# Two branch projections of a decoder trunk, rebuilt from seven half-size products each and moved behind all gates

## The chip, the cores and the metric

One core of a Trainium2 chip runs the whole kernel. The metric is device time in microseconds (us). TensorE (PE) multiplies matrices into PSUM; VectorE (DVE), ScalarE (ACT) and GpSimd (POOL) do the elementwise work; SyncE (SP), ACT and POOL issue the transfers between HBM and SBUF, each from a queue of its own. Every engine works through its own list of instructions in order, and waits where an operand of the next one isn't there yet.

## The reference

One layer of a hybrid decoder trunk, with 1024 tokens and a model width of 1024, in float32:

```
h = RMSNorm(x);  P = h @ W_in
y_0 = RWKV-7 recurrence over P   (8 heads x 64)
y_1 = stick-breaking attention   (8 heads x 64)
y_2 = cross attention into 256 memory tokens (4 heads x 128)
merged = sum_b sigmoid(G_b) * (y_b @ W_br[b])     b = 0, 1, 2
x += merged @ W_out
x += ConvFFN(RMSNorm(x))
```

Each `y_b` is 1024 tokens x 512, each `W_br[b]` 512 x 1024, and the gates `G_b` are 3 x 1024 columns of P. The change concerns the lines with `merged` for b = 1 and 2.

## The kernel before

All tensors lie transposed, 128 features on the partitions and 1024 tokens along the free dimension. Matrix products keep float32 accuracy by splitting each operand into a high part (an ACT copy to the type fp32r) and a low part (a subtraction on DVE or POOL), and by three matmuls in place of one: high x high, high x low, low x high. PE works on up to 128x128 weights and 512 columns at a time, and a matmul stands in the profile as one LDWEIGHTS (PEld) and one MATMUL of `mmul`, line 139.

The program is written as Python generators, and their interleaving sets PE's order. A *main* generator (a recurrence, an attention) is woven with a *filler* stream of projections: `weave(main, filler, ratio)` advances the main part by one step and the filler by `ratio` units on average. A unit of filler is what stands between two of its `yield`s, most often six matmuls. `pinned` keeps an instruction in program order on its engine, and while `strict` is set, each pinned instruction also comes behind the pinned one before it on that engine. What isn't pinned (the copies that end a gate, most weight splits, stores) is placed by the scheduler.

The part that the change rewrites is the strict part, in which the main generator is `stage2`, the recurrence over 16 chunks of 64 tokens. Each chunk has three thirds, each one step: A makes small products for eight heads, which DVE copies (L656); B multiplies these by the chunk's inverse, and ACT copies the results (L664); C makes the output, copied by ACT (L676), and the new state, updated by DVE (L674). Each third needs the copies of the third before it. After chunks 3, 7, 11, 13 and 15 (counted from zero) `norm_part` adds the group norm in pieces to the following steps: reductions on DVE (L699, L700), squares on ACT (L706, four a step, 16 for a part of two groups and 8 for a part of one), a power on POOL (L195), and scalings on DVE (L715). `group_norm` follows with the ratio 1.0: it transposes on PE (`turn`, L729 and L730 on DVE) and splits the result (L734 on ACT, L735 on DVE). Then comes `branch_last`, the projection for b = 0.

The filler in that part: `gate_item` (eight units of six matmuls; `fin` copies on ACT L885 and scales on DVE L886; the sigmoid L889 is put off to the next item's unit by `close_gates`, and the gate goes to HBM in `gsd`), and `branch_item` (four units; DVE multiplies the product by the gate, L1297; for b = 2 POOL adds the sum so far, L1299; POOL issues the store to `mrd`, L1300). The mark `y1`, three gates after the memory attention, starts it. Before, 20 of the 24 gates go to HBM and four stay on the chip beside their branch item; the items after the mark are the eight of branch 1, one gate with the splits of branch 2's operand, the eight of branch 2 with a gate before each of the last four, and two gates. Gates and old sums share three buffers of the tag `w4`; loads come from SP (L1283, L1286).

The later parts that the change touches: in `up_phase`, the up projection, which is already made with seven products of half size for eight, `act_sums` adds activation blocks on DVE (the tile `gall`); in `down_phase`, `complete` adds finished output blocks (L1874) at the start of each group of steps; in `sb_qk`, `k_split` copies the keys' halves.

## Time and profile before

| | us |
|---|---|
| median of three runs (lowest, highest) | 1789.28 (1788.69, 1789.63) |
| profiled execution, own time | 1788.33 |
| its span, first to last instruction | 1786.6 |
| PE busy in the span | 1774.7 |
| DVE / ACT / POOL busy | 1185.1 / 883.3 / 698.3 |

The span is 1.7 us shorter than the profiled execution's own time; the rest lies around the instructions. Stretches of the profile are given in us from the span's start. The strict part with the recurrence runs from about 779 to 985, the group norm to about 1009, the up projection to about 1490, and the down projection to the end. PE's busy time counts overlapping matmuls once; the start-to-start distance of the matmuls is their cost.

### The profile page before, as it was taken

To read this page: it belongs to the slowest core of one execution; us is meant where nothing else is said; L and a number is where in the kernel's file an instruction comes from. 1 tells how busy PE (TensorE), PEld (TensorE's weight loads), DVE (VectorE), ACT (ScalarE), POOL (GpSimd) and SP (SyncE) were. 2 spreads that over 40 slices of the span, in tenths; PEclk is the share of its full clock that TensorE was granted. 3 is DMA by queue.
4 is the path that set the end of the run, shared out by engine and by line. 5 is a ranking of instruction groups with operands and counts; after the bars stand their busy time and mean duration, and the time that the engine had idled before them with its cause. 6 is when DMAs were issued, how large, how long until landed. Compare 5 with 4: busy or idle time off the path is not lost.

```text
span 1786.6 us, 27452 instructions
## 1 busy us (share of the span) xinstructions
PE 1774.7 (99%) x10481; PEld 1442.4 (81%) x10481; DVE 1185.1 (66%) x1687; ACT 883.3 (49%) x1667; POOL 698.3 (39%) x409
## 2 busy tenths in 40 slices
PE   9999999999999999999999999999999999999999
PEld 7777778878888888787777888887888888888887
DVE  5666674787888655243533873698767777795597
ACT  6544344566566635444546434454444445445343
POOL 1233252222231012122433321257777677535454
PEclk9999999999999999999999999999999999999999
DMA  4256574111112333658763653323323333396475
GB/s 185 74 166 193 181 244 148 51 57 42 54 57 77 103 126 93 203 181 278 269 228 145 230 211 105 108 89 124 101 89 104 115 104 113 109 329 224 142 246 202
DMA packets 120757, 263.39 MB, mean 147 GB/s; under 512 B 28329, under 2 KB 41129, under 8 KB 120498
## 3 DMA queue, kind: packets, MB, share of 16 engines
q1 hardware_dynamic: 82434, 193.31, 33.1%
q10 hardware_dynamic: 34416, 55.72, 8.5%
q0 software_dynamic: 3776, 12.62, 2.3%
q8 instruction: 82, 1.34, 0.3%
q14 instruction: 49, 0.40, 0.1%
HBM read 180.04 MB, written 81.53 MB: 146 GB/s over the span
## 4 chain that ended last, share of the span: by engine, by line
PE 61%; issue 1%; DVE 1%; POOL 1%; ACT 1%; DMA 1%; ACTq 0%; DVEq 0%; POOLq 0%; SPq 0%
PE mm L139 53%; PE g L139 8%; PE g L122 1%; POOL dw L1854 1%; DMA vmd<-w 0%; ACT wh L83 0%; DMA qk<-vd 0%; DVE qk L715 0%; ACT w L885 0%; DVE gall L1646 0%; DVE w L886 0%; DVE ga L1635 0%; DVE keep L1874 0%; DVE g L1629 0%; DVE g L1630 0%
## 5 line engine op out<-in xcount | busy, mean ns | idle before, releaser
L89 POOL TENSOR_TENSOR wl<-wr,wh 128x1024 fp32r<-128x1024 f32 x58 | 147.8, 2550 | 368.2 <-ACT wh L83 355.0
L139 PE MATMUL mm<-xhi,wh 128*128 128x512 f32 x784 | 260.5, 413 | 1.4 <-ACT xhi L222 1.0
L139 PE MATMUL mm<-xlo,wh 128*128 128x512 f32 x784 | 243.6, 392 | 0.1
L139 PE MATMUL mm<-xhi,wl 128*128 128x512 f32 x784 | 242.2, 390 | 0.0
L139 PEld LDWEIGHTS mm<-xlo,wh 128*128 128x128 f32 x784 | 147.0, 188 | 33.4 <-DVE xlo L225 1.0
L139 PEld LDWEIGHTS mm<-xhi,wl 128*128 128x128 f32 x784 | 147.2, 188 | 32.7
L139 PEld LDWEIGHTS mm<-xhi,wh 128*128 128x128 f32 x784 | 136.6, 189 | 31.1 <-issue 7.9
L139 PE MATMUL mm<-dw,da 128*128 128x512 f32 x528 | 120.9, 390 | 0.0
L83 ACT ACTIVATE wh<-wr 128x1024 fp32r<-128x1024 f32 x75 | 79.5, 1060 | 81.5 <-PE mm L139 57.2
L139 PE MATMUL mm<-BT,l 128*128 128x512 f32 x504 | 117.9, 389 | 0.3 <-POOL l L1555 0.3
L139 PEld LDWEIGHTS mm<-dw,da 128*128 128x128 f32 x528 | 98.9, 188 | 21.3 <-DVE da L1853 0.8
L1854 POOL TENSOR_TENSOR dw<-draw,dw 128x512 fp32r<-128x512 f32 x55 | 83.6, 1530 | 76.1 <-ACT dw L1852 74.2
L985 DVE TENSOR_TENSOR_SCAN at<-at,at 128x128 f32<-128x128 f32 (+3 forms) x64 | 91.0, 1428 | 33.1 <-ACT at L979 33.0
L139 PEld LDWEIGHTS mm<-BT,l 128*128 128x128 f32 x504 | 94.5, 188 | 20.3 <-POOL l L1555 0.7
L139 PE MATMUL mm<-BT,wh 128*128 128x512 f32 x352 | 108.6, 390 | 1.7 <-DVE u L1685 1.7
L139 PE MATMUL mm<-B,wh 128*128 128x512 f32 x352 | 108.6, 389 | 0.0
L195 POOL TENSOR_TENSOR hf<-rs,half 128x16 f32<-128x16 f32 (+1 forms) x18 | 49.2, 2734 | 142.2 <-DVE rs L192 137.8
L1853 DVE TENSOR_TENSOR da<-draw,da 128x512 fp32r<-128x512 f32 x77 | 66.9, 877 | 49.1 <-ACT da L1851 48.8
L139 PE MATMUL g<-dw,da 128*128 128x512 f32 x396 | 90.6, 389 | 0.4 <-POOL dw L1854 0.4
L1851 ACT ACTIVATE da<-draw 128x512 fp32r<-128x512 f32 x77 | 48.3, 628 | 80.7 <-PE mm L139 29.9
L139 PEld LDWEIGHTS g<-dw,da 128*128 128x128 f32 x396 | 74.2, 188 | 16.2 <-POOL dw L1854 0.8
L1555 POOL TENSOR_TENSOR l<-it,l 128x1024 fp32r<-128x1024 f32 x20 | 48.0, 2402 | 85.5 <-ACT l L1554 85.5
(343 smaller groups left out, 3972.1 us busy)
## 6 DMA issues: line engine op xcount, KB each, us to landing
wr<-in_w_in_dram SPq DMA_DIRECT2D x49, 512.0 KB, 3.7
draw<-actd SPq DMA_DIRECT2D x77, 256.0 KB, 3.3
at<-scr SPq DMA_DIRECT2D x28, 512.0 KB, 5.6
draw<-in_w_down_dram SPq DMA_DIRECT2D x55, 256.0 KB, 4.8
rw<-in_w_up_dram SPq DMA_DIRECT2D x22, 512.0 KB, 3.6
actd<-gall ACTq DMA_DIRECT2D x41, 256.0 KB, 3.4
gsd<-w ACTq DMA_DIRECT2D x20, 512.0 KB, 2.7
wr<-in_w_up_dram SPq DMA_DIRECT2D x18, 512.0 KB, 3.6
```

What stands on the lines that cost most here:

```text
L83: ins = self.nc.scalar.activation(hi, raw, AF.Copy)
L89: self.last_wl = self.nc.gpsimd.tensor_tensor(lo, raw, hi.bitcast(F32), ALU.subtract)
L122: self.pinned(self.nc.tensor.transpose(out, in_, self.ident[:n, :n]))
L139: self.pinned(self.nc.tensor.matmul(*a, **k))
L195: nc.gpsimd.tensor_tensor(out, t[:, :n], self.half[:, :n], ALU.pow)
L985: self.pinned(nc.vector.tensor_tensor_scan(sn[:, :W][:, ::-1], sn[:, :W][:, ::-1], self.smask[:, 1024 - W :][:, ::-1], 1.0, ALU.mult, ALU. ...
L1555: self.last_low = keep(eng.tensor_tensor(lo, src, hi.bitcast(F32), ALU.subtract))
L1851: self.pinned(nc.scalar.activation(A[:, 0], a, AF.Copy))
L1853: self.pinned(nc.vector.tensor_tensor(A[:, 1], a, A[:, 0].bitcast(F32), ALU.subtract))
L1854: nc.gpsimd.tensor_tensor(Wt[:, 1], w, Wt[:, 0].bitcast(F32), ALU.subtract)
```

## The change

For a pair of row blocks (256 output features) and one branch, the old code makes two blocks of 128 features x 1024 tokens with K = 512. The new `branch_pairs` cuts the pair's weight into four blocks `a11, a12, a21, a22` (by half of K and by row block) and the operand `y` into four blocks by half of K and half of the tokens, and makes the four output blocks from seven products of half size (2 k x 3 = 6 matmuls of 512 columns each) for eight. It needs sums of weights (on POOL: three per pair ahead, and `a12` minus a sum later), sums of operand blocks (on DVE, four of 128x1024 per branch), the splits of seven operands per branch (14 for two, where eight tiles were split), splits of each product's weight (56 of 256 columns, high on ACT and low on POOL, seven products ahead), a copy of the first product out of PSUM on ACT, and joins of the products on DVE. All of these are pinned. `st["t"]` and `st["o"]` hold joins and old sums; `xt` gives the operands the buffers of `xhi` and `xlo`, which the last gate frees piece by piece.

The order becomes: all seven gates left behind the mark `y1`, the last two with hooks (`hooks1`, `hooks2`) that make the operands of branch 1 and the first weights; then 56 products, one unit each. Branch 2's operands are made during products 21 to 31. The filler ratio goes from 2.08 to 1.92. All 24 gates now go to HBM, and each product pair loads its two gates back.

Also: the copies in `k_split` come behind the last copy that ends a gate; the memory keys take two `at` buffers in place of `w4`; in the up projection the activation sums of one pair move from the end of its own third product and the next pair's sixth to the next pair's sixth and seventh; in the down projection the additions after the group with i = 7 (done in the group with i = 4) are spread over every second step, 0 to 6, and the stores come at step 8.

```diff
...
     def t4(self, tag="w4", dt=F32, n=1024):
...
+
+    def xt(self, name, dt=F32R):
+        return self.pool_x.tile([128, 1024], dt, name=self.nm(name), tag="xt", bufs=16)
...
     def ps(self, tag="g"):
...
-        self.xhi, self.xlo = ([self.pool_x.tile([128, 1024], F32R, name=f"x{n}{k}") for k in range(8)] for n in ("hi", "lo"))
+        self.xhi, self.xlo = zip(*[[self.xt(f"x{n}{k}") for n in ("hi", "lo")] for k in range(8)])
...
         def load(eng, tile, src):
...
-        self.rbc = self.pool_x.tile([128, 1024], F32, name="rbc")
+        self.rbc = self.pool_x.tile([128, 1024], F32, name="rbc", tag="rbc", bufs=1)
...
-            nc.scalar.activation(K[i][q], kr[q], AF.Copy)
-            nc.scalar.activation(K[i][o], kr[q], AF.Copy)
+            for x in (q, o):
+                self.behind(nc.scalar.activation(K[i][x], kr[q], AF.Copy), self.last_fin)
...
-                st["k"] = self.t4(), self.t4()
+                st["k"] = self.t4("at"), self.t4("at")
...
-    def load_y(self, b, st):
...
     def branch_mm(self, d, w, y, out, k):
...
-    def branch_item(self, b, d, st, first):
...
-    def branch(self, b, first):
...
+    def branch_pairs(self):
+        nc = self.nc
+        act = lambda *a, **k: self.pinned(nc.scalar.activation(*a, **k))
+        vec = lambda o, a, b, op: self.pinned(nc.vector.tensor_tensor(o, a, b, op))
+        gps = lambda o, a, b, op: self.pinned(nc.gpsimd.tensor_tensor(o, a, b, op))
+        f = lambda x: x.bitcast(F32)
+        two = lambda x: x.rearrange("p (k t) -> p k t", k=2)
+        N, L, R = 8, slice(0, 512), slice(512, 1024)
+        seq = [(0, 1)]
+        for n in range(N):
+            seq += [(n, 6), (n, 2), (n, 5), (n, 7), (n, 4)] + ([(n + 1, 1)] if n + 1 < N else []) + [(n, 3)]
+        at = {x: s for s, x in enumerate(seq)}
+        st, Y, W, S, G, bank, wh, wl, raws, early = {}, {}, {}, {}, {}, {}, [], [], {}, []
+
+        def load_y(b, tiles):
+            raws[b] = [two(t) for t in tiles]
+            for q, (k, t) in zip(raws[b], ((0, L), (0, R), (2, L), (2, R))):
+                nc.sync.dma_start(f(q), self.yd[b, k : k + 2, :, t].rearrange("k p t -> p k t"))
+
+        def load_first():
+            load_y(1, [self.t4("A", dt) for dt in (F32, F32, F32, F32R)])
+
+        def operands(b):
+            q11, q12, q21, q22 = raws[b]
+            if b == 1:
+                st["big"] = self.pool_a.tile([128, 4, 1024], F32R, name="yhi", tag="inst")
+            big = [two(st["big"][:, j]) for j in range(4)]
+            new = lambda dt=F32R: two(early.pop(0) if early else self.xt("y", dt))
+            low = lambda: two(self.t4("A", F32R)) if b == 1 else new()
+            sub = lambda o, x, y: vec(o, x, y, ALU.subtract)
+
+            def split(i, q, hi, lo):
+                act(hi, f(q), AF.Copy)
+                sub(lo, f(q), f(hi))
+                Y[b, i] = hi, lo
+
+            yield split(1, q11, big[0], big[1])
+            yield sub(q11, q12, q11)
+            yield split(2, q21, big[2], big[3])
+            t2 = st["t2"] = new(F32)
+            sub(t2, f(q22), q11)
+            yield sub(q21, t2, q21)
+            yield split(6, t2, new(), new())
+            yield split(5, q11, new(), new())
+            yield sub(q12, f(q22), q12)
+            yield split(7, q12, new(), low())
+            hi4, hi22 = new(), new()
+            yield split(4, q21, hi4, low())
+            yield split(3, q22, hi22, q22)
+
+        def tiles(*dts):
+            early.extend(self.xt("y", dt) for dt in dts)
+
+        def begin():
+            st["y"] = operands(1)
+            next(st["y"])
+
+        def load_w(n):
+            if n < N:
+                W[n] = self.load_w(self.I["w_br"][1 + n // 4, n % 4])
+
+        def quads(n):
+            w = W[n].rearrange("p (a k m c) -> p m a k c", a=2, k=2, m=2)
+            return w[:, 0, 0], w[:, 0, 1], w[:, 1, 0], w[:, 1, 1]
+
+        def weight_sums(n):
+            if n < N:
+                a11, a12, a21, a22 = quads(n)
+                s1, s2 = S[n] = [st["s"][:, n % 2 * 512 + o : n % 2 * 512 + o + 256].rearrange("p (k c) -> p k c", k=2) for o in (0, 256)]
+                gps(s1, a21, a22, ALU.add)
+                gps(s2, s1, a11, ALU.subtract)
+                gps(a21, a11, a21, ALU.subtract)
+
+        def operand(s, tile, k=None):
+            x = tile[s % 8 // 4][:, s % 4 * 256 : s % 4 * 256 + 256]
+            return x.rearrange("p (k c) -> p k c", k=2) if k is None else x[:, k * 128 : (k + 1) * 128]
+
+        def weight(s):
+            if s >= len(seq):
+                return
+            n, i = seq[s]
+            a11, a12, a21, a22 = quads(n)
+            if i == 3:
+                gps(a12, a12, S[n][1], ALU.subtract)
+            src = {1: a11, 2: a12, 3: a12, 4: a22, 5: S[n][0], 6: S[n][1], 7: a21}[i]
+            hi, lo = operand(s, wh), operand(s, wl)
+            act(hi, src, AF.Copy)
+            gps(lo, src, f(hi), ALU.subtract)
+
+        def room():
+            wh.append(self.pool_wt.tile([128, 1024], F32R, name=self.nm("wh"), tag="wh", bufs=2))
+            wl.append(self.pool_wt.tile([128, 1024], F32R, name=self.nm("wl"), tag="wl", bufs=2))
+
+        def w_first():
+            room()
+            load_w(0)
+
+        def w_next():
+            load_w(1)
+
+        def gate(n, r):
+            if n < N:
+                g = G[n, r] = self.t4()
+                nc.sync.dma_start(g, self.gsd[1 + n // 4, n % 4 * 2 + r])
+
+        def old(n, r):
+            if n < N and "o" in st:
+                nc.sync.dma_start(st["o"][n % 2 * 2 + r], self.mrd[n % 4 * 2 + r])
+
+        def put(n, r):
+            g, d = G.pop((n, r)), n % 4 * 2 + r
+            if n > 3:
+                (nc.vector if n == N - 1 else nc.gpsimd).tensor_tensor(g, g, st["o"][n % 2 * 2 + r], ALU.add)
+            nc.gpsimd.dma_start(self.mrd[d], g)
+
+        def product(s):
+            n, i = seq[s]
+            key, first = {1: ("A", True), 2: ("A", False), 6: ("B", True), 7: ("B", False), 5: ("C", True), 3: ("C", False), 4: ("D", True)}[i]
+            if first:
+                bank[n, key] = self.ps("mm")
+            o, y = bank[n, key], Y[1 + n // 4, i]
+            for k in range(2):
+                for pi, (u, v) in enumerate(((0, 0), (0, 1), (1, 0))):
+                    self.mmul(o, operand(s, (wh, wl)[u], k), y[v][:, k], start=(first and k == 0 and pi == 0),
+                              stop=(k == 1 and pi == 2), skip_group_check=not first)
+            p1 = st["t"][0][:, L] if n % 2 else st["t"][1][:, L]
+            x2, x3 = st["t"][0][:, R], st["t"][1][:, R]
+            if i == 1:
+                act(p1, o, AF.Copy)
+            elif i == 6:
+                vec(x2, o, p1, ALU.add)
+            elif i == 5:
+                g = G[n, 0]
+                vec(g[:, L], bank.pop((n, "A")), g[:, L], ALU.mult)
+            elif i == 7:
+                vec(p1, o, p1, ALU.add)
+                vec(x3, bank[n, "C"], p1, ALU.add)
+            elif i == 4:
+                vec(p1, p1, o, ALU.subtract)
+                g = G[n, 1]
+                vec(g[:, L], p1, g[:, L], ALU.mult)
+                vec(g[:, R], x3, g[:, R], ALU.mult)
+                put(n, 1)
+                gate(n + 1, 0)
+                old(n + 2, 1)
+            elif i == 3:
+                vec(x2, o, x2, ALU.add)
+                g = G[n, 0]
+                vec(g[:, R], x2, g[:, R], ALU.mult)
+                put(n, 0)
+                gate(n + 2, 1)
+                old(n + 2, 0)
+
+        def run():
+            yield
+            gate(0, 1)
+            gate(0, 0)
+            room()
+            st["t"] = [self.pool_x.tile([128, 1024], F32, name=self.nm("rbc"), tag="rbc", bufs=1), st["x"]]
+            for s in range(4, 7):
+                weight(s)
+            for s in range(len(seq)):
+                product(s)
+                n, i = seq[s]
+                weight(s + 7)
+                if s == 0:
+                    self.close_gates()
+                    gate(1, 1)
+                if s % 7 == 1:
+                    load_w(s // 7 + 2)
+                if s % 7 == 5:
+                    weight_sums(s // 7 + 2)
+                if s in (0, 2):
+                    next(st["y"])
+                if s == 1:
+                    load_y(2, [self.xt("q", dt) for dt in (F32, F32, F32, F32R)])
+                elif s == 20:
+                    st["y"] = operands(2)
+                elif 21 <= s <= 31 and s != 27:
+                    next(st["y"])
+                if s == 31:
+                    st["o"] = [x.rearrange("p k t -> p (k t)") for x in (*raws[2][:3], st["t2"])]
+                    for r in (1, 0):
+                        old(4, r)
+                        old(5, r)
+                yield
+
+        def sums_first():
+            st["x"], st["s"] = self.xt("t", F32), self.xt("s", F32)
+            weight_sums(0)
+
+        step = lambda: next(st["y"])
+        weights = lambda *ss: lambda: [weight(s) for s in ss]
+        hook = lambda *fs: lambda: [g() for g in fs]
+        hooks1 = {1: begin, 3: step, 5: step}
+        hooks2 = {0: hook(w_first, lambda: tiles(F32, F32R)), 1: hook(step, w_next, lambda: tiles(F32R, F32R)), 2: hook(step, lambda: tiles(F32R, F32R)),
+                  3: hook(step, lambda: tiles(F32R, F32R)), 4: sums_first, 5: hook(step, weights(0, 1)), 6: hook(step, weights(2, 3)), 7: lambda: weight_sums(1)}
+        return load_first, hooks1, hooks2, run()
...
     def load_wo(self, k):
...
-                if n > 2 and pairs[n - 1][2]:
-                    act_sums(pairs[n - 1][1], True)
...
-                elif pairs[n][2]:
-                    act_sums(pairs[n][1], False)
...
         def u1_first(n):
...
-                    late, part = ((False, 0), (False, 1), (True, 0), (True, 1))[(5, 6, 7, 4).index(i)]
-                    act_sums(0, late, (part,))
+                    for late, part in {5: ((False, 0),), 6: ((False, 1), (True, 0)), 7: ((True, 1),)}.get(i, ()):
+                        act_sums(0, late, (part,))
+                elif n > 3 and n % 2 == 0 and i in (6, 7):
+                    act_sums(pairs[n - 1][1], i == 7)
...
-            if f < 4:
+            if i != 4 and f < 4:
...
-            elif f == 5:
+            elif i == 4 and f < 8 and f % 2 == 0:
+                complete(f // 2)
+            elif f == (8 if i == 4 else 5):
...
-        self.stored = set(gq)
+        gq += [(2, d) for d in range(4, 8)]
...
-        ld1, br1, sp1 = self.branch(1, True)
-        ld2, br2, sp2 = self.branch(2, False)
-        items += [lambda: drain(inv), ld1, gate(sp1), gate(), gate(), mark("y1"), *br1, ld2, gate(sp2), *br2, gate(), gate()]
+        load1, hooks1, hooks2, pairs = self.branch_pairs()
+        items += [lambda: drain(inv), load1, gate(), gate(), gate(), mark("y1"), *[gate() for _ in range(5)], gate(hooks1), gate(hooks2), pairs]
...
-        self.weave(st2, pump, 2.08, 0)
+        self.weave(st2, pump, 1.92, 0)
...
```

46 lines of the change are left out of this document (1 added, 45 removed).

## The prediction

> **What bounds the kernel now.** I read the page first, then busy time by stretch, then the instructions in order of time in the stretch that the change rewrites, then the groups by form that give each price.
>
> ```profile
> span 1786.6 us, 27452 instructions
> PE 1774.7 (99%) x10481; PEld 1442.4 (81%) x10481; DVE 1185.1 (66%) x1687; ACT 883.3 (49%) x1667; POOL 698.3 (39%) x409
> 779.00:985.00 206.00, 205.28 (x2110) 161.41 (x2109) 86.28 (x245) 111.23 (x405) 67.05 (x39) 1.00 0.65 227
> 1200.00:1480.00 280.00, 278.01 (x1225) 229.58 (x1224) 210.41 (x312) 130.02 (x179) 208.20 (x121) 1.00 0.33 107
> 1480.00:1786.00 306.00, 302.39 (x1329) 248.77 (x1328) 225.55 (x280) 134.19 (x218) 163.45 (x106) 1.00 0.58 196
> ```
>
> PE is the bound: 1774.7 of 1786.6 us busy, and in the stretch 779 to 985, where both branch projections run between the thirds of the recurrence's chunks, 205.28 of 206. The clock column says 1.00 throughout. A matmul taken away saves its time if nothing else becomes late. DVE (86 us) and ACT (111 us) have room there on average; whether they have it at each step decides this change.
>
> ```profile
> 780.83 0.61 PE L139 MATMUL mm<-yhi,wh 128*128 128x512 f32 x2
> 782.19 0.61 PE L139 MATMUL mm<-yhi,wh 128*128 128x512 f32 x2
> 796.15 0.68 PE L139 MATMUL g<-ys,at 64*64 64x64 f32 x16
> 800.18 0.68 PE L139 MATMUL g<-ys,qk 64*64 64x64 f32 x16
> 803.74 0.68 PE L139 MATMUL g<-ys,at 64*64 64x64 f32 x16
> 808.40 0.56 PE L139 MATMUL g<-ys,at 64*64 64x64 f32 x12
> ```
>
> A unit of filler is six matmuls and takes 782.19 - 780.83 = 1.36 us, 0.227 each. The other rows are one chunk's thirds (A, B, C) with two units behind each: 4.03, 3.56 and 4.66 us.
>
> **The change part by part.** *Matmuls.* Two branches x 8 row blocks x 24 = 384 become 56 products x 6 = 336. 48 x 0.227 = 10.9 us saved; nothing else on PE changes.
>
> *Moved activation sums, spread additions, key buffers.*
>
> ```profile
> 1239.65 0.73 PE L139 MATMUL mm<-BT,wh 128*128 128x512 f32 x2 [1.69 <-DVE u L1685]
> 1741.88 10.99 PE L139 MATMUL g<-dw,da 128*128 128x512 f32 x47 [0.36 <-POOL dw L1854]
> ```
>
> These are the two waits there that the moved DVE work can cause. Removed, they give 2.0; not removed, 0. I take 1.5. The order of the key copies and the `at` tiles I cost at nothing, since PE's rows cover them.
>
> *What ACT and DVE get.* The prices, from two views: rows that begin with a line number are groups (busy us, mean ns of one | idle before, what ended it), rows that begin with a time are single stretches in order (start, length, in brackets the idle time before).
>
> ```profile
> L885 ACT ACTIVATE w<-mm 128x512 f32<-128x512 f32 x15 | 8.2, 593 | 0.1
> L889 ACT ACTIVATE w<-w 128x1024 f32<-128x1024 f32 x8 | 8.5, 1058 | 13.8 <-DVE w L886 13.8
> L1365 ACT ACTIVATE mg<-at 128x256 fp32r<-128x256 f32 x16 | 5.8, 408 | 2.2 <-DVE at L1359 2.2
> 777.45 2.96 ACT L1267 ACTIVATE yhi<-A 128x1024 fp32r<-128x1024 f32 x3 [0.40 <-ACT w L889]
> 886.83 0.35 ACT L706 ACTIVATE jk<-qk,hn 128x64 f32<-128x64 f32 x1 [4.09 <-DVE hn L700]
> 887.30 0.35 ACT L706 ACTIVATE jk<-qk,hn 128x64 f32<-128x64 f32 x1
> 888.71 1.86 ACT L664 ACTIVATE qk<-g 64x64 f32<-64x64 f32 x8
> L1297 DVE TENSOR_TENSOR w<-mm,w 128x512 f32<-128x512 f32 x32 | 20.5, 683 | 17.9 <-PE mm L139 13.6 <-DMA w<-gsd 4.3
> L715 DVE TENSOR_SCALAR qk<-qk,hn,hf 128x64 f32<-128x64 f32 x64 | 17.1, 336 | 0.9 <-POOL hf L195 0.9
> L674 DVE SCALAR_TENSOR_TENSOR ys<-ys,pc,g 128x64 f32<-128x64 f32 x60 | 14.5, 279 | 50.4 <-issue 25.5 <-PE g L139 25.0
> L656 DVE COPY ys<-g 128x64 f32<-128x64 f32 x64 | 9.8, 214 | 21.8 <-PE g L139 21.8
> 743.51 1.22 DVE L886 TENSOR_TENSOR w<-w,rbc 128x1024 f32<-128x1024 f32 x1 [10.27 <-ACT w L885]
> ```
>
> Back to back, ACT's 128x1024 copies take 2.96/3 = 0.99, a square 0.47 (887.30 - 886.83), eight recurrence copies 1.86. From 1.06 to 0.99 is 0.1 of overlap, so a 512 copy is 0.5 and a 256 copy (a weight's high part) 0.31. On DVE a 512 operation that reads PSUM is 0.68 (0.66 in a row), a 1024 one 1.22.
>
> In the strict part every pinned instruction keeps program order on its engine, and the new splits, copies and additions are all pinned, so a late one holds up the recurrence's copies behind it, on which the next third's matmuls wait. After the mark y1 come 7 gates of 8 units, then 56 products. At 1.92 units a step the last gate falls on steps 26 to 30 and product s on step (57+s)/1.92; the group norm's squares (four a step) sit on steps 28-31, 40-43 and 46-47 as before.
>
> *Stretch 1, steps 26-31* (thirds C A B C A B, the first with one unit). PE: 3.30+4.03+3.56+4.66+4.03+3.56 = 23.1. ACT: four sets of recurrence copies 7.4, 16 squares 7.5, four operand splits 4.0, two gates' copies 2.1 and sigmoids 2.1, eight weights 2.5, one product copy 0.5: 26.1. ACT is 3.0 behind when the next C third needs its copies; and it idles at the start, as the 4.09 in the 886.83 row shows for the same place now: the first split there waits for DVE, which has a gate's scaling, the reductions and a sum ahead of it. Ends: 1.5 (the last copies may trail) and 8; I take 3.0+4.1 = 7.
>
> *Stretch 2, steps 40-47, products 18-33.* PE 3x3.56+3x4.66+2x4.03 = 32.7. DVE: 23 joins 15.2 (nine per seven products), eleven 1024 operations for branch 2's operands 13.2, the recurrence 2x4x0.214+3x4x0.279 = 5.1, 16 scalings 5.4: 38.9, so 6.2 over. ACT: 24 squares 11.3, six sets of copies 11.2, 16 weights 5.0, seven splits 6.9, two product copies 1.0: 35.4, 2.7 over. They wait on each other (split, low part, split) and two norm parts start, each with the 4 us wait. Ends: 3 (ACT's excess alone) and 17 (both excesses and two waits); I take 12.
>
> *Stretch 3, the group norm, 15 units.*
>
> ```profile
> 986.32 1.03 PE L122 MATMUL g<-kon,qk 128*128 128x128 f32 x8
> 987.11 0.71 PE L139 MATMUL mm<-xhi,wh 128*128 128x512 f32 x2
> L729 DVE TENSOR_TENSOR at<-g,at 128x512 f32<-128x512 f32 x7 | 4.7, 684 | 1.3 <-PE g L122 1.3
> L735 DVE TENSOR_TENSOR A<-qk,qk 128x512 fp32r<-128x512 f32 x6 | 4.0, 684 | 0.1
> ```
>
> PE: 15x1.36 plus 32 transposes at 0.79 per eight, 23.6. DVE: 24 operations of 0.684 (16.4), eight scalings 2.7, 15 x 9/7 joins 12.7: 31.8, against gates there now. 8 behind, less what the last projection's start can wait. Ends 1 and 12; I take 6.
>
> *POOL and the gates' loads.*
>
> ```profile
> L1299 POOL TENSOR_TENSOR w<-w,w 128x1024 f32<-128x1024 f32 x7 | 16.6, 2378 | 25.7 <-DVE w L1297 20.6 <-DVE hn L699 3.5 <-DMA w<-mrd 1.6
> L1582 POOL TENSOR_TENSOR wr<-wr,wr 128x512 f32<-128x512 f32 x10 | 12.9, 1287 | 0.0
> L1300 POOL DMA_DIRECT2D mrd<-w x16: 531/572/616, 787.5 to 997.8; - x16
> DMA to landing us min/median/max: 2.9/5.8/7.9
> L1283 SPq DMA_DIRECT2D w<-gsd x12: 319/319/320, 765.8 to 887.1; - x12
> DMA to landing us min/median/max: 3.3/4.1/4.8
> 891.61 1.29 DVE L1297 TENSOR_TENSOR w<-mm,w 128x512 f32<-128x512 f32 x2 [4.30 <-DMA w<-gsd]
> ```
>
> POOL gets 56 low parts and 32 sums of 256 columns; no such row exists, and the line through 1.29 and 2.38 gives 0.75: 66 us over the phase. A low part is made seven products (9.5 us of PE) ahead of its use, so I cost POOL's time itself at nothing; but the high parts of four kinds in seven are taken from POOL's sums, so a late POOL makes ACT wait, in front of the recurrence's copies. Each pair's second gate loads into the buffer that the pair before stores from: three DVE joins 2.0, issue 0.57, landing 5.8, load 0.32+4.1 = 12.8, and 15.2 with the addition, against five products and two to three thirds, 6.8+3.5 = 10.3. DVE then waits 2.5 or 4.9; a 4.30 wait at 891.61 cost PE nothing. On SP a waiting gate load holds the recurrence's and the weights' next loads; the former are asked for two groups (four chunks) ahead, the latter almost two pairs, so some 5 us cost them nothing. Ends 0 and 10; I take 2. The four gates that are newly stored and read back add four store issues on ACT's queue and four loads on SP's, beside PE's work: nothing.
>
> **Sum.** -10.9 - 1.5 + 7 + 12 + 6 + 2 = +14.6. On the profiled run's 1788.33 that is 1802.9; the median, 1789.28, stands 1 us higher: 1804. All at the good ends -13 (1776); at the bad ones 8+17+12+10-10.9 = +36 (1825).
>
> **Rivals.** *Faster: the backlog is absorbed.* A recurrence copy is needed only one step later, so 2.7 us of lateness is free, and the real order of the unpinned gate copies may be kinder. If ACT and DVE never fall more than one step's two units behind in any stretch, only the saving is left: -12.4, 1777. For it: the 4.30 wait without cost. Against it: the excesses of 3 to 8 us. It decides where ACT's 26.1 us in stretch 1 shrink below 23.1+2.7.
>
> *DVE is locked out by POOL.*
>
> ```profile
> 980.33 2.40 POOL L89 TENSOR_TENSOR wl<-wr,wh 128x1024 fp32r<-128x1024 f32 x1 [9.18 <-ACT wh L83]
> 981.46 2.35 DVE L886 TENSOR_TENSOR w<-w,rbc 128x1024 f32<-128x1024 f32 x1 [8.08 <-ACT w L885]
> ```
>
> The operation that took 1.22 at 743.51 took 2.35 here: it got almost nowhere until POOL ended at 982.73. POOL would be busy some 20 of stretch 2's 32.7 us (16 low parts and 11 sums of 0.75), six tenths of it, and 19 of DVE's larger operations there (eleven for the operands, eight gate products) have both inputs in SBUF. If six tenths of them meet a POOL operation and lose 0.75 each, DVE is 8 us later: +23, 1812. [...]
>
> *The gate loads rule.* If each of the seven rounds stops PE for its wait, 4x2.5+3x4.9 = 25 in place of the stretches' delays, which would run inside those waits: -12.4+25 = +12, 1801. Against it: the 4.30 wait.
>
> **Chances.** The forecast 0.40, the lock 0.13, the gate loads 0.07 (all slower); absorbed, 0.30; half absorbed, stalls between 9 and 16 us, within 0.2% (3.6 us, about what a measurement of this kernel can tell from no change), 0.10. Faster 0.30, same 0.10, slower 0.60. The range 1776 to 1825 holds both signs; the likeliest case alone is 1796 to 1814.
>
> **What would show it.** PE's records fall by 48 and its idle time in the rewritten stretch rises from under 1 us to some 27, as waits for ACT's recurrence copies (L664, L676) near the last gate and for DVE's copies and updates around branch 2's splits; ACT over 0.9 busy there. Wrong would be: PE idle below 12 us in all, or waits that name DMA or POOL first. In the up projection the 1.69 wait should be gone.

## The result and the profile after

The changed kernel takes 1865.53 us (median of 5 runs, 1864.86 to 1867.82), the kernel before 1789.28 beside it: a ratio of 1.0426 (95% interval 1.0411 to 1.0442), 76 us slower. The forecast was 1804, with a range up to 1825: the sign was right, the size was not.

The page of the changed kernel, the whole span: busy time of each engine, and the granted clock of PE in 40 slices.

```profile
span 1863.8 us, 27582 instructions
PE 1796.1 (96%) x10433; PEld 1451.6 (78%) x10433; DVE 1266.3 (68%) x1742; ACT 900.5 (48%) x1729; POOL 753.7 (40%) x488
PEclk9999999999999999999888799999999999999999
```

PE's records fell from 10481 to 10433: the 48 matmuls are gone. The clock has a dent that the page before did not show. Busy time by stretch (start:end, length, then busy time and instructions of PE, PEld, DVE, ACT and POOL, PE's clock, DMA share, GB/s):

```profile
779.00:985.00 206.00, 186.40 (x1863) 143.78 (x1861) 102.20 (x223) 116.90 (x401) 74.21 (x71) 0.95 0.53 187
985.00:1085.00 100.00, 66.56 (x347) 51.60 (x348) 75.80 (x123) 34.39 (x103) 55.77 (x53) 0.78 0.56 197
```

Up to 985 PE idles 20 us where it idled 0.7, from 985 to 1085 another 33. The last projection, `branch_last`, starts at 1081.6 in place of 1011.8: 70 of the 76 us are lost here, in the stretch that the change rewrites. What PE waits for between 779 and 1090 (engine, tile and line <- releaser: us in total, times, longest; lines of the changed kernel: L667 and L679 are the copies of the second and last thirds, L659 DVE's copies, L1262 to L1264 the new helpers on ACT, DVE and POOL):

```profile
PE g L142 <- ACT qk L667: 14.5, 3, 7.2
PE mm L142 <- DVE rbc L1263: 11.2, 2, 6.4
PE g L142 <- DVE ys L659: 9.2, 3, 6.3
PE mm L142 <- DVE t L1263: 8.6, 2, 5.9
PE g L142 <- ACT qk L679: 7.2, 4, 5.6
```

The first large wait, beside the last gate, and the start of the last projection:

```profile
908.37 1.90 PE L142 MATMUL g<-ys,at 64*64 64x64 f32 x16 [7.23 <-ACT qk L667]
...
1081.61 1.23 PE L142 MATMUL mm<-qk,wh 128*128 128x512 f32 x4
```

Some 31 of the 51 us of waits look like the forecast's picture (ACT's and DVE's copies late), 20 are waits of the products for DVE's joins. ACT itself, in the same stretch, does not lack time (116.9 of 206 us busy, and 13.3 of 18 from 890 to 908 beside the last gate, where the forecast had over 0.9); it waits:

```profile
ACT wh L1262 <- POOL wr L1264: 57.8, 8, 11.4
ACT qk L679 <- DVE ys L677: 19.8, 11, 3.3
```

One of these eight waits in single stretches (start, length, in brackets the idle time before), POOL, ACT and PE in order of time:

```profile
1013.04 2.34 POOL L1372 TENSOR_TENSOR w<-w,q 128x1024 f32<-128x1024 f32 x1
...
1017.37 0.57 POOL L1373 DMA_DIRECT2D mrd<-w  x1
1017.96 0.74 POOL L1264 TENSOR_TENSOR wr<-wr,s 128x256 f32<-128x256 f32 x1
1018.73 0.42 ACT L1262 ACTIVATE wh<-wr 128x256 fp32r<-128x256 f32 x1 [9.38 <-POOL wr L1264]
1019.06 1.85 ACT L667 ACTIVATE qk<-g 64x64 f32<-64x64 f32 x8
1019.54 1.42 PE L142 MATMUL g<-ys,at 64*64 64x64 f32 x12 [6.20 <-ACT qk L667]
```

POOL adds an old sum, makes two weight sums and a low part of other products (the rows left out), issues the store, and only then subtracts `s2` from `a12` for the weight of the third kind. ACT has waited 9.38 us for that subtraction; the recurrence's copies stand behind the weight on ACT, and PE waits 6.20 us for the copies. POOL, which the prediction costed at nothing, is at the head of this chain. Another of PE's waits for ACT is of the same kind:

```profile
945.64 0.42 ACT L1262 ACTIVATE wh<-wr 128x256 fp32r<-128x256 f32 x1 [8.35 <-POOL wr L1264]
946.58 1.89 PE L142 MATMUL g<-ys,at 64*64 64x64 f32 x16 [5.59 <-ACT qk L679]
```

### The profile page after: what moved, and what is told of

Same layout as the page of the kernel before. It is cut to its first block, busy times and chain, and to the rows that moved or that the text cites. A ratio compares the mean times of both kernels' runs of the same rounds, so it can differ in the third digit from the quotient of the medians.

```text
span 1863.8 us, 27582 instructions
## 1 busy us (share of the span) xinstructions
PE 1796.1 (96%) x10433; PEld 1451.6 (78%) x10433; DVE 1266.3 (68%) x1742; ACT 900.5 (48%) x1729; POOL 753.7 (40%) x488
## 4 chain that ended last, share of the span: by engine, by line
PE 47%; DVE 7%; issue 5%; ACT 4%; POOL 3%; DMA 1%; SPq 0%; ACTq 0%; DVEq 0%; POOLq 0%
PE mm L142 40%; PE g L142 6%; POOL dw L1999 1%; DVE gall L1793 1%; ACT g L1774 1%; PE g L125 1%; DVE gall L1782 1%; ACT sg L1779 1%; DVE qk L718 1%; POOL wl L1264 1%; DVE qk L733 1%; DVE g L1777 1%; DVE w L1263 1%; DVE rbc L1263 0%; ACT jk L709 0%
## 5 line engine op out<-in xcount | busy, mean ns | idle before, releaser
L92 POOL TENSOR_TENSOR wl<-wr,wh 128x1024 fp32r<-128x1024 f32 x50 | 128.9, 2578 | 346.5 <-ACT wh L86 340.9
L86 ACT ACTIVATE wh<-wr 128x1024 fp32r<-128x1024 f32 x67 | 71.1, 1061 | 79.4 <-PE mm L142 74.9
L1774 ACT ACTIVATE g<-u,params 128x512 f32<-128x512 f32 x88 | 64.9, 770 | 68.8 <-DVE u L1853 63.5
```

The source lines that it names most:

```text
L86: ins = self.nc.scalar.activation(hi, raw, AF.Copy)
L92: self.last_wl = self.nc.gpsimd.tensor_tensor(lo, raw, hi.bitcast(F32), ALU.subtract)
L1774: keep(nc.scalar.activation(c, u[:, 2 + h * 512 : 514 + h * 512], AF.Identity, scale=self.par("cw2", m), bias=self.par("cb", m)))
```

## The experiments

All times below are medians (the kernel before, run beside each group, stood between 1788.9 and 1790.1, so a difference of 1 us between two groups says nothing); "the base" is the kernel of the third run, 1852.33, on which most of the others are built. Two theories were set against each other: Q, the order of POOL's queue, and L, that DVE and ACT have too much to do, as forecast, only more of it. A third, P, came up after the first four.

| run | edit | us | ratio to before, 95% interval |
|---|---|---|---|
| e1 | third-kind sum made earlier | 1856.32 | 1.0371 (1.0357, 1.0385) |
| e2 | stores issued by SP | 1861.11 | 1.0394 (1.0378, 1.0410) |
| e3 | both: the base | 1852.33 | 1.0351 (1.0337, 1.0365) |
| e4 | kernel before + small edits | 1796.08 | 1.0036 (1.0023, 1.0048) |
| e5 | base, no POOL low parts | 1841.33 | 1.0292 (1.0277, 1.0307) |
| e6 | base, low parts on DVE | 1849.21 | 1.0338 (1.0322, 1.0353) |
| e7 | base, low parts and sums on DVE | 1851.18 | 1.0348 (1.0333, 1.0363) |
| e8 | base, norm's scalings on ACT | 1851.14 | 1.0345 (1.0327, 1.0362) |
| e9 | base, no POOL arithmetic in the products | 1829.66 | 1.0220 (1.0202, 1.0238) |
| e10 | base, no DVE work for branch 2's operands | 1843.19 | 1.0299 (1.0283, 1.0315) |
| e11 | base, ratio 1.6 | 1853.21 | 1.0352 (1.0335, 1.0368) |
| e12 | base, ratio 2.3 | 1854.69 | 1.0367 (1.0348, 1.0385) |
| e13 | base, matmuls repeated at the waits | 1852.71 | 1.0352 (1.0338, 1.0366) |
| e14 | base, two of the norm's three DVE steps out | 1848.19 | 1.0328 (1.0312, 1.0344) |
| e15 | kernel before + moved activation sums | 1795.96 | 1.0034 (1.0021, 1.0046) |
| e16 | kernel before + spread additions | 1789.89 | 1.0003 (0.9995, 1.0012) |
| e17 | e9 + e10 + e14 | 1815.11 | 1.0145 (1.0128, 1.0162) |
| e18 | e17 without the gates' loads | 1802.14 | 1.0070 (1.0055, 1.0085) |

**e1, e2, e3: POOL's queue.**

```diff
-            if i == 3:
-                gps(a12, a12, S[n][1], ALU.subtract)
+            if i == 5:
+                gps(a11, a12, S[n][1], ALU.subtract)
...
-            src = {1: a11, 2: a12, 3: a12, ...
+            src = {1: a11, 2: a12, 3: a11, ...
```

> The sum a12 - s2 for the third-kind weight is made four products earlier (into a11, which is free by then), so that ACT's high part no longer waits for a POOL queue with the stores and additions of the pair before in front. Nothing else changes. Theory Q (queues: ACT waits 57.8 us in 8 waits for POOL, POOL waits for DVE's joins, and the recurrence's copies stand behind ACT's wait): most of the stalls go, PE idles below 25 us between 900 and 1085 in place of about 55, the clock there rises above 0.92, and the time is 1800 to 1820. Theory L (load: ACT and DVE simply have more to do than PE around the last gate and branch 2's operands, as the prediction had it, with terms too small): the ACT waits for POOL vanish, but PE's idle time stays above 40 us and the time is 1850 to 1866.

The second kernel leaves that as it was and moves the stores:

```diff
-            nc.gpsimd.dma_start(self.mrd[d], g)
+            nc.sync.dma_start(self.mrd[d], g)
```

> The stores of the finished pairs are issued by SP in place of POOL; POOL keeps the additions of the last three pairs. Theory Q: POOL no longer waits for DVE's joins in the first four pairs, so the first four of the eight ACT waits shrink from 3 to 8 us to below 2 each; the additions still hold POOL from pair 4 on: 1825 to 1850. Theory L: no change within 5 us of 1865. SP's loads now stand behind stores that wait for DVE: if that matters, waits that name DMA on the w4 tiles appear, and the time rises.

> Both edits. Theory Q: the earlier sum alone already uncouples ACT from the stores, so this stands within 5 us of the early sum alone. Theory L: within 5 us of 1865.

The order of the queue costs 9.2 us, the stores' place another 4.0; together 13.2, a sixth of the loss. The first two times lie 36 and 11 us above theory Q's ranges and within theory L's; the third, within 5 us of the first, is Q's, and 8 us below L's range. So Q holds for a part, not in its full form: after the first edit ACT's waits for POOL shrink from 57.8 us to 12.1 (of which none is for the third kind's sum), and PE waits for DVE instead. The rows after the first edit, PE, DVE and POOL, show by whom DVE was held:

```profile
1025.45 0.79 PE L142 MATMUL mm<-y,wh 128*128 128x512 f32 x1 [8.77 <-DVE t L1263]
1026.04 0.63 PE L142 MATMUL mm<-q,wh 128*128 128x512 f32 x1
1026.47 0.63 PE L142 MATMUL mm<-y,wl 128*128 128x512 f32 x1
...
1047.85 2.38 POOL L1372 TENSOR_TENSOR w<-w,q 128x1024 f32<-128x1024 f32 x1 [1.24 <-DVE w L1263]
1048.72 0.68 DVE L732 TENSOR_TENSOR at<-g,at 128x512 f32<-128x512 f32 x1
...
1050.70 4.73 DVE L733 TENSOR_TENSOR qk<-at,at 128x512 f32<-128x512 f32 x1
1051.12 1.44 POOL L1264 TENSOR_TENSOR wl<-wr,wh 128x256 fp32r<-128x256 f32 x2
1052.52 2.36 POOL L1372 TENSOR_TENSOR w<-w,q 128x1024 f32<-128x1024 f32 x1
```

An addition of 128x512 with both inputs in SBUF (0.69 us on average in the kernel before) took 4.73 and ended at 1055.43, 0.55 us after POOL's run of three operations. An operation of the same size that reads PSUM (the tile `g`) took 0.68 beside POOL's addition of 2.38. A DVE held by POOL is the rival that the prediction gave 13%; it became theory P. The rows also show PE's matmuls 0.43 us apart after the wait of 8.77, where 0.23 is their distance in the kernel before, at a granted clock of 1.00.

**e5 to e9: what POOL's arithmetic costs.** In e5 the low parts after the first eight are left out; e6 gives the low parts to DVE, e7 the sums too; e9 leaves out the low parts after the first eight, the sums from the third pair on, and POOL's additions of old sums.

```diff
-            gps(lo, src, f(hi), ALU.subtract)
+            if s < 8:                                   # e5, e9
+                gps(lo, src, f(hi), ALU.subtract)
+            vec(lo, src, f(hi), ALU.subtract)           # e6, e7
...
-                gps(s1, a21, a22, ALU.add)
+                vec(s1, a21, a22, ALU.add)              # e7, and the other sums
```

> From the kernel with the earlier sum and SP's stores: POOL's low parts of the weights after the first eight are left out (the old ones stay in their buffers), so the output isn't the reference's, and 48 POOL operations of 128x256 go. Everything else, DVE's and ACT's work too, stays. Theory P (POOL locks DVE out: in the trace with the earlier sum, one 128x512 group-norm addition took 4.73 us at 1050.70 in place of 0.68, ending with a run of POOL operations; such excesses over the unhindered lengths sum to some 33 us between 900 and 1085): the excess falls to below 18 us, PE idles less by 10 to 20 us, and the time is 1815 to 1840. Theory L (DVE and ACT have too much work of their own, whatever POOL does): 1846 to 1853.

> The same kernel with the 56 low parts made by DVE in place of POOL. DVE gets 56 x 0.37 = 20 us more, spread over the 56 products. Theory P: what DVE gets it wins back from the lock, 1840 to 1860. Theory L: DVE is 20 us busier in stretches where it sets the pace, 1860 to 1875.

> Low parts and weight sums all on DVE; POOL keeps the additions of old sums alone. DVE gets 31 us more. Theory P: 1838 to 1865, with DVE's excess over its unhindered lengths below 10 us. Theory L: 1868 to 1885.

> From the kernel with the earlier sum and SP's stores, like the run without low parts, but POOL's weight sums from the third pair on and its additions of old sums are left out as well (the output isn't the reference's); POOL is left with the small powers of the norm, the first splits, the transfers it issues and the last projection's splits. Theory P (the lock): DVE's operations keep their unhindered lengths up to the last projection and the time falls by as much again as without the low parts, to 1820 to 1833. Theory L (DVE's own load): within 4 us of the run without low parts, 1837 to 1845.

POOL's arithmetic costs 22.7 us (e9 against the base), the low parts alone 11.0: theory P's range holds three of the four times and misses e5 by 1 us; theory L's holds none. Moved to DVE, 20 and 31 us of added work (by the expectations' count) cost nothing on balance (-3.1 and -1.2): DVE won back about what it was given. Its groups show it; first the changed kernel, then the base, then the kernel with all of it on DVE, each from 900 to 1085:

```profile
L718 DVE TENSOR_SCALAR qk<-qk,hn,hf 128x64 f32<-128x64 f32 x48 | 21.1, 509 | 0.0
L733 DVE TENSOR_TENSOR qk<-at,at 128x512 f32<-128x512 f32 x6 | 11.3, 1891 | 0.0
```

```profile
L718 DVE TENSOR_SCALAR qk<-qk,hn,hf 128x64 f32<-128x64 f32 x48 | 15.6, 397 | 0.0
L733 DVE TENSOR_TENSOR qk<-at,at 128x512 f32<-128x512 f32 x6 | 6.7, 1127 | 0.0
```

```profile
L718 DVE TENSOR_SCALAR qk<-qk,hn,hf 128x64 f32<-128x64 f32 x48 | 11.2, 308 | 0.0
L733 DVE TENSOR_TENSOR qk<-at,at 128x512 f32<-128x512 f32 x6 | 5.6, 944 | 0.0
```

The scalings take 509, 397 and 308 ns (306 in e9, 305 in the kernel before), the additions 1891, 1127 and 944: POOL's arithmetic accounts for the second step, the first came with the order of its queue. That DVE's operations run longer beside POOL's arithmetic is shown by these rows; that all 22.7 us are this lock is not, since without POOL's work its queue and the additions between join and store are gone as well. From the base to e9 the scalings, these additions and the norm's low parts (L738) lose 8.9 us of busy time in this window.

**e8, e11, e12: the same work on another engine or at another time.**

```diff
-                self.pinned(nc.vector.tensor_scalar(y, y, nm[:, j : j + 1], rs[:, j : j + 1], ALU.add, ALU.mult))
+                self.pinned(nc.scalar.activation(y, y, AF.Identity, bias=nb[:, j : j + 1], scale=rs[:, j : j + 1]))   # e8; nb = nm * rs
...
-        self.weave(st2, pump, 1.92, 0)
+        self.weave(st2, pump, 1.6, 0)      # e11; e12: 2.3
```

> The group norm's 64 scalings made by ACT (Identity with scale and bias, some 0.35 us each) in place of DVE (19.4 us for 48 of them between 900 and 1085 where unhindered ones take 11.3). Both theories that put the stalls on DVE: 1830 to 1845. If ACT is the engine that sets the pace (its 22 us more fall where it has the squares and the recurrence's copies): 1855 to 1870.

> From the same kernel with 1.6 units of filler a step in place of 1.92: more of the recurrence and the group norm's first parts fall on the gates, where DVE is busy 50 of 121 us, fewer on the products. If DVE's joint load of joins, operands and norm is what stalls PE: 1830 to 1847. If the thirds' own latency needs the 2.6 us of filler behind each: stalls from 785 on that name the recurrence's copies, 1855 to 1880.

> From the same kernel with 2.3 units a step: the recurrence is spread over more products, fewer products beside the group norm. By the joint load the stalls get fewer in 940 to 1022 and the recurrence's end runs longer: 1845 to 1865. If the products themselves (joins, gate loads) set the pace, no change within 4 us.

All three lie within 2.4 us of the base; the first two fit neither of their expectations, the third fits both and so decides nothing. With the scalings on ACT, PE's waits for DVE's copies fall from 8.4 us in the base to 1.2 and those for the joins in `t` from 14.4 to 10.5, but those for ACT's copies, 3.4 in the base, become:

```profile
PE g L142 <- ACT qk L667: 11.8, 5, 3.9
```

Most of what DVE was relieved of, ACT charged: in this run neither engine alone sets the pace.

**e10, e14: the two loads that the prediction had costed.** In e10 `sub` does nothing for b = 2 and high parts serve as low ones; in e14 this goes:

```diff
-            sub = lambda o, x, y: vec(o, x, y, ALU.subtract)
+            sub = lambda o, x, y: vec(o, x, y, ALU.subtract) if b == 1 else None        # e10
...
-            self.pinned(nc.vector.tensor_tensor(y[:, hs], gg[:, hs], bg[:, hs], ALU.add))      # e14
...
-            nc.vector.tensor_tensor(lo[:, hs], self.y[p][:, hs], hi[:, hs].bitcast(F32), ALU.subtract)      # e14
```

> From the same kernel with DVE's eleven 128x1024 operations for branch 2's operands left out (high parts serve as low parts, unsummed blocks as sums, so the output isn't the reference's); ACT's seven copies stay. The prediction put 13.2 us of DVE work and a stall of 12 us there. Theory L: 1832 to 1843. If the stall there comes from elsewhere (the lock, the gate loads, ACT): 1848 to 1853.

> From the same kernel: the group norm's additions (eight of 128x512) and low parts (eight) on DVE are left out in the stretch after the recurrence, and high parts stand in for low ones in the last projection (the output isn't the reference's). The prediction had DVE 8 us behind PE there, and a cost of 6. If DVE's own load sets that stretch: 16 x 0.68 = 11 us and what the lock adds, 1832 to 1842. If the stalls there come from elsewhere (loads of the old sums, POOL's additions): 1847 to 1853.

They give 9.1 us, at the upper edge of theory L's range, and 4.1, which says that the stalls behind the recurrence come from elsewhere too. In the second, DVE's waits show what comes next, the gate loads: two waits in the base (first row), four without the norm's steps (second), both from 895 to 1082.

```profile
DVE w L1263 <- DMA w<-gsd: 11.2, 2, 6.1
```

```profile
DVE w L1261 <- DMA w<-gsd: 20.9, 4, 8.1
```

**e13: the slower clock.**

```diff
+            if s in (42, 46, 55):
+                idle = self.ps("g")
+                for _ in range(24):
+                    self.mmul(idle, *self.again, start=True, stop=True)
+            self.again = operand(s, wh, 0), y[0][:, 0]
...
+            for _ in range(40 if c == 14 else 0):
+                self.mmul(us[0][7][:, 256:512], self.again[0], self.again[1][:, :256], start=True, stop=True)
```

> From the kernel with the earlier sum and SP's stores: repeated matmuls, whose results nobody reads, are put in front of the four places where PE waits 6 to 8 us (the second third of the recurrence's chunk 14 and products 42, 46 and 55), 24 of 512 columns (5.4 us) or 40 of 256 (some 4.7 us) each, so that PE works in most of each wait. Theory K (the slower clock after a wait costs by itself: six matmuls take 2.55 us in place of 1.36 behind the wait that ended at 1025 in the trace with the earlier sum): the clock rises above 0.94 between 985 and 1070 and the time falls to 1838 to 1847. If DVE sets the pace there whatever PE's speed: 1850 to 1856, with PE's waits behind the added matmuls longer.

Busy time by stretch, the base and then this kernel:

```profile
985.00:1022.00 37.00, 27.51 (x214) 20.62 (x213) 19.01 (x43) 21.38 (x82) 19.73 (x19) 0.87 0.55 202
1022.00:1066.00 44.00, 26.73 (x102) 20.83 (x101) 38.51 (x51) 10.33 (x19) 26.81 (x20) 0.77 0.55 203
```

```profile
985.00:1022.00 37.00, 34.10 (x279) 27.43 (x278) 16.97 (x40) 19.70 (x78) 17.87 (x18) 0.98 0.55 200
1022.00:1066.00 44.00, 34.75 (x149) 27.82 (x150) 39.70 (x52) 11.07 (x22) 28.75 (x21) 0.95 0.55 203
```

The clock rose from 0.87 and 0.77 to 0.98 and 0.95, and the time did not move (+0.4 us). At products 42, 46 and 55 PE still waits behind the repeats (1.5, 3.6 and 2.5 us): there DVE and the loads set the pace, and a slow PE only waits less. The fourth group, in the recurrence's chunk 14, came behind its wait and held PE itself:

```profile
980.89 7.53 PE L142 MATMUL g<-y,wh 128*128 128x256 f32 x40 [6.21 <-DVE ys L659]
988.35 0.68 PE L142 MATMUL g<-ys,qk 64*64 64x64 f32 x16
```

Product 55 starts 1.3 us later than in the base, so a gain of that size from the faster clock could be hidden. Matmuls stand 0.43 us apart behind waits of 8.77 (e1), 3.17 (e18, below) and 3.62 (here, at product 46), and 0.23 apart behind the one of 1.49 at product 42. In this stretch the slower clock costs at most some 2 us of its own (an estimate: the 1.3 and the scatter of the runs).

**e4, e15, e16: the small edits on the kernel before.** The edits are those of the change itself, without `branch_pairs`; the first has all of them, the others one each:

```diff
-                if n > 2 and pairs[n - 1][2]:
-                    act_sums(pairs[n - 1][1], True)                  # e15
...
+                elif n > 3 and n % 2 == 0 and i in (6, 7):
+                    act_sums(pairs[n - 1][1], i == 7)                # e15
...
-            if f < 4:
+            if i != 4 and f < 4:
                 complete(f)
+            elif i == 4 and f < 8 and f % 2 == 0:
+                complete(f // 2)                                     # e16
```

> The kernel before with the small edits alone (order of the key copies, key buffers, moved activation sums, spread additions), without the seven-product branches. The prediction has -1.5: 1787.5 to 1788.2. By the changed kernel's trace, where the up projection's small waits for DVE's u sum to 4.3 us and 1.5 more for POOL's l while the one of 1.69 is gone, they cost 1 to 4 us: 1790 to 1793.

> The kernel before with the moved activation sums alone. The four small edits together cost 6.0 us. By the trace of those, where DVE's u makes eight waits in place of one and POOL's l one more, nearly all of it is this: +3 to +6, 1792 to 1796. By the prediction: -1.7, 1787.6.

> The kernel before with the spread additions of the down projection alone. By the trace of the four small edits PE's busy time after 1480 changed by 1.3 us: within 1.5 us of before, 1788 to 1791. By the prediction -0.4.

The small edits cost 6.0 us, more than either reading had; the moved activation sums alone 6.0, the spread additions nothing. PE's waits with the moved sums alone, the largest two:

```profile
PE mm L139 <- DVE u L1618: 4.4, 8, 0.6
PE mm L139 <- POOL l L1555: 1.5, 1, 1.5
```

The one wait of 1.69 has become eight of up to 0.6, and one of POOL's grew from 0.3 to 1.5: 3.9 us of the 6.0. The other 2 have no row; PE's busy time is longer too, 1778.0 us where the page of the kernel before has 1774.7 for the same 10481 matmuls, and why stays open.

**e17, e18: all at once.** e17 joins e9, e10 and e14. e18 also leaves the gates' loads out:

```diff
-                g = G[n, r] = self.t4()
-                nc.sync.dma_start(g, self.gsd[1 + n // 4, n % 4 * 2 + r])
+                G[n, r] = self.t4()
...
-                vec(g[:, L], bank.pop((n, "A")), g[:, L], ALU.mult)
+                vec(g[:, L], bank.pop((n, "A")), f(st["big"][:, 0])[:, L], ALU.mult)
```

> From the kernel with the earlier sum and SP's stores, three things left out at once: POOL's low parts, sums and additions, DVE's operations for branch 2's operands, and DVE's additions and low parts of the group norm (the output isn't the reference's). If the causes add up: 1852.3 - 22.7 - 9.1 - 4.1 = 1816. If they cover each other and the gate loads come last: DVE waits over 20 us for gate loads between 900 and 1050 and the time is 1810 to 1825. If they cover each other without the gate loads: 1785 to 1808, with DVE's waits for loads below 12 us.

> The same without the gates' loads: the products are multiplied by another tile that stays on the chip, and the buffer that takes the result is still the one that the pair before stores from. If the gate loads were the last bound: within 6 us of the floor, 1789.5 + 6.0 (small edits) - 10.9 (48 matmuls) = 1785, with PE's waits between 900 and 1050 below 8 us. If a cause without a name is left: over 1797.

The three parts add up: 37.2 us together, 35.9 one by one (22.7 + 9.1 + 4.1). That the gate waits would grow past 20 us was wrong (11.8 us in four, PE's waits 16 in all), but their loads are worth 13.0 us once the rest is gone. What is left in e18, 17.5 us above the floor of 1784.6 (1789.5 + 6.0 - 10.9), is only partly named: as its expectation says for a time over 1797, a cause without a name is left. PE's waits, and the rows around the largest (one of ACT among them):

```profile
PE g L142 <- ACT qk L667: 3.6, 2, 3.2
PE mm L142 <- DVE t L1261: 1.7, 2, 1.5
PE g L142 <- DVE ys L659: 1.4, 1, 1.4
```

```profile
904.38 1.85 ACT L667 ACTIVATE qk<-g 64x64 f32<-64x64 f32 x8
904.86 1.90 PE L142 MATMUL g<-ys,at 64*64 64x64 f32 x16 [3.17 <-ACT qk L667]
906.69 1.97 PE L142 MATMUL g<-qk,at 128*64 128x64 f32 x32
...
910.89 0.63 PE L142 MATMUL mm<-y,wl 128*128 128x512 f32 x1
911.32 0.63 PE L142 MATMUL mm<-y,wh 128*128 128x512 f32 x1
...
912.59 0.40 PE L142 MATMUL mm<-A,wh 128*128 128x512 f32 x1
912.83 0.40 PE L142 MATMUL mm<-y,wl 128*128 128x512 f32 x1
913.15 0.56 PE L142 MATMUL g<-ys,at 64*64 64x64 f32 x12
```

This is the wait beside the last gate. Behind it the products' matmuls stand 0.43 us apart (910.89, 911.32), and 0.24 at 912.59; the granted clock is 0.91 from 900 to 940, with 1.00 in the stretches before and behind. Here PE is the bound again, so that costs: by the distances of the rows some 3.4 us (an estimate: 1.2 and 0.8 on the two groups of the third, 7 matmuls by 0.2). A part of the 1.2 may belong to ACT's eight copies, which run beside that group and which it needs. The pages bound the rest: against the kernel with the small edits (span 1794.3, PE busy 1778.8) e18 (1799.1 and 1774.8) has 8.8 us more idle time of PE and, with 10.9 of matmuls gone, 6.9 more busy time than these leave. Waits of 7.5 and the slow stretch of 3.4 are named; the other 5, and some 2 between these profiled runs and the medians, no run here explains.

## Why the prediction was wrong

By its own terms, in its order:

- *Matmuls, -10.9.* The 48 are gone. Their worth cannot be read off alone, since PE is no longer the bound in that stretch.
- *Moved activation sums and spread additions, -1.5.* Measured +6.0, all of it the moved sums (e15). The wait was rightly found and did go; the DVE work that moved made eight others. The working asked which wait goes, not what is late next.
- *Stretch 1, +7.* The C third behind the last gate waited 7.23 us for ACT's copies, as forecast, but that the number agrees is luck. More than half of it was POOL's: with the sum made earlier the wait is 3.17 (e1), about the 3.0 by which the working had ACT behind. With the slow matmuls after it some 6.6 stay in e18.
- *Stretch 2, +12.* PE's waits in these steps sum to 11.0 us, and DVE's operand work is worth 9.1 (e10). About right; what ACT's excess and the two norm waits, the rest of the term, were worth no run separates.
- *Stretch 3, +6.* Too small: here PE waited 19.8 us for DVE's joins. The norm's two steps are worth only 4.1 of what was lost (e14); the lock and the gates' loads, priced elsewhere or at little, are in the rest.
- *Gates' loads, +2.* The loop was worked out rightly at 12.8 to 15.2 us and then taken for covered. It is, partly, by the other stalls; without them it is worth 13.0 (e18 against e17).
- *POOL's time, "at nothing".* This is the step that failed. The order of POOL's queue costs 13.2 (e3), its arithmetic 22.7 (e9): 35.9 of the 61.5 us by which the time lies above the forecast. The prediction even named the chain (a late POOL makes ACT wait, in front of the recurrence's copies), but looked at POOL's average load and at a lead of seven products, not at what stands before the one subtraction that has no lead over ACT's copy: low parts and sums for other products, and the store and the addition of the pair before, which wait for DVE's joins. The waits of 5.59 and 6.20 us, which lie outside all three stretches of the forecast, and some 4 of the 7.23 come from it. And the lock, kept out of the sum as a rival, was priced at 0.75 us an operation for six tenths of 19 operations with both inputs in SBUF, 8 us. That the others stay free of it was not shown: the norm's scalings were longer too (397 ns in the base, 306 in e9), and one operation of 4.73 us went on through three of POOL's (e1).

Of the rivals, the absorbed backlog (1777) is refuted; the lock (1812) and the gates' loads (1801) were both there, beside the others and not in place of them. The prediction took them as alternatives; the runs show a sum. From the changed kernel to e18, 63.4 us are the queue 13.2, the three parts 37.2 and the loads 13.0. From e18 to the kernel before, 12.6 are +6.0, -10.9 and the 17.5 of which some 7 stay open.

What would show it wrong was named rightly: waits that name DMA or POOL first. They do, but on ACT and DVE, one step behind PE; PE's own waits alone do not show it.

The low end of the range doesn't follow from the working either: with the good ends that it gives (1.5, 3, 1 and 0, and -2.0) the sum is -7.4 us, 1782. The -13 (1776) has every stall at nothing.

## What to carry to other kernels

An engine off the critical path is not free because its share is low: look in its queue for the one instruction that another engine waits for, and at what stands in front of it. Where POOL is to work beside DVE, ask what it costs DVE. Here the norm's scalings took 397 ns in the base and 306 in e9 and its additions 1127 and 932, while the joins that read PSUM kept their 0.68 us and the reductions of 128x128 their 0.27; POOL's own time would have been an upper bound (an estimate: e5's expectation counts some 33 us of excess in e1 between 900 and 1085, and POOL's operations there sum to some 104). And delays that look like alternatives can add up: a change that loads four engines in one stretch should be priced by the sum of its stalls, with the clock's loss counted mainly where PE is the bound (where DVE and the loads set the pace, 0.95 to 0.98 in place of 0.77 to 0.87 changed the time by 0.4 us, e13).

## What was not expected of the hardware

- A DVE addition with two SBUF inputs took 4.73 us in place of 0.69, through three POOL operations in a row (e1), and scalings of 128x64 took 397 ns on average in the base where 306 without POOL's arithmetic (e9). By the profile's starts, DVE's addition was 0.42 us ahead of the first of the three.
- PE's clock could be kept at 0.95 to 0.98 through waits by repeated matmuls, where it was 0.77 to 0.87, without any gain in time that these runs can show, in a stretch where DVE and the loads set the pace.
